# TensorE held to the program's order in layer 0, and sums of squares by head with the squares moving

## The chip, the cores and the metric

The kernel runs on one core of one Trainium2 chip. The metric is the device time of one execution in microseconds (us), the median of three runs. The trace is one profiled execution. Engines are named as in the profile: PE is TensorE's matmuls and PEld its weight loads, DVE is VectorE, ACT ScalarE, POOL GpSimd, SP SyncE; a q behind a name (ACTq, SPq) is the engine's queue, which issues DMAs. L12 is line 12 of the kernel before.

## The reference, cut to what matters

A first block of two layers works on x (256 tokens, width 1024): windowed attention (even layer), then latent attention with rotary keys (odd layer), a final RMS norm. A second block of two layers then works on x and on a context ctx of 256 tokens. In each of its layers:

- an RMS norm over the width and a modulation computed from c;
- q, k and v; **q and k are normalised per head half** (64 channels), the attention's output per head (128 channels), so sums of squares by head are needed;
- differential attention, x over x and ctx; a pooling and a convolution branch; gates; an output projection;
- an expert layer (`peer_ffn`): 8 heads each choose 16 of 16384 experts by two top-16 lists over 128 keys; `gelu(x . u_e)` times the gate weighs the row `v_e`.

```python
def rms_norm(x, g):
    xf = x.astype(jnp.float32)
    y = xf * lax.rsqrt(jnp.mean(xf * xf, axis=-1, keepdims=True) + EPS)
    return (y * g.astype(jnp.float32)).astype(x.dtype)

def qk_heads(p, g):
    b, l = p.shape[:2]
    return rms_norm(p.reshape(b, l, N_HEADS, 2, HEAD_DIM), g)

def attn_out_norm(o, g, lam_init):
    b, l = o.shape[:2]
    return (rms_norm(o, g) * (1.0 - lam_init)).reshape(b, l, ATTN_W)
```

## The kernel before, in words

**Layout.** Activations lie transposed: channels on the 128 partitions, 256 tokens along the free axis, eight chunks for 1024 channels. Most matrices come in chunks of 128x1024 (512 KB). `WS` (L253) loads each by DMA (L268), splits it into a high part (`wa`, ACT, L281) and a low part (`wb`, DVE, L282), up to LEAD chunks ahead, and `mm3` (L405) multiplies with three passes (high x high, high x low, low x high): 24 matmuls a chunk at L409 to L411. Chunks named in `whole` are not split and take 8 matmuls in full precision (`mm1`, L413, L416).

**Order of the work.** The program is a set of Python generators. Each yields a number of units, roughly its share of time, and combinators interleave them: `lead` (L1654) runs side generators by a rate against the main one, `par` (L1623) shares by weights, `along` (L1679) steps a side once per unit over a rate, `until` (L1671) runs a generator up to a `yield None`. What they settle is the order of writing. The framework then **schedules**: for each engine, DMA queues included, it plays the program on a model of the chip and picks the next instruction among those that are ready by that model, earlier-written ones first. It also assigns the buffers (42 of 4 KB under the tag `pg`) in that order. The order on an engine is fixed before the run; on the chip each engine works through its own.

**Stages.** `program` (L1699) starts with x's first norm (in `b1`, L693), ctx's norm and the first modulation matmuls (`mods`, L537, L574). Then two streams run side by side under `lead`, ctx at twice x's units (RATE[0]): x goes through the first block (`b1`), then layer 0's mixer; ctx goes through its mixer (`mixer`, L1160: `qkv`, `attn2`, branches, output), its choice of experts (`topk`, L1223), layer 1's modulation, and from about 860 us on through `rows` (L1351): each chosen expert's row is gathered by an indirect DMA (L1381), multiplied and added on DVE (L1392, L1401); 512 such rows, paced by units. At 1290 us x's mixer ends and `ffn_start` (L1690) begins: 24 steps (SOLO) of the choice alone, then under `par` the rest of the choice, the **G tables** (`gbuild`, L1470: one-hot products per token, L1487 and L1489 on DVE, L1495 on PE, written to DRAM at L1504 from ACT's queue) and the first 20 chunks of expert matrix u (`peer`, L1507, up to its `yield None`; 16 in full precision, four split: NPRE). A full-precision chunk counts 256/75 = 3.41 units, a split one 256/100 = 2.56. From 1560 to 2300 us `peer`'s main loop takes 128 chunks of u (the first ones done) and v. Layer 1 follows in the same pattern without ctx's mixer.

**Norms.** `rms_bcast` (L464) squares on ACT (L472), sums over channels with PE: ones as 32-column weights, squares moving, chunk k of four into the 32 output partitions of column group k (L474). A copy (L476), two matmuls by token (L479), the reciprocal root on DVE (`rsqrt`, 13 small operations, L396 to L403), a diagonal tile (L498) and a product with ones (L501) spread it over the partitions. The sums **by head** go another way: in `qkv` (L946) and `attn2` (L1046) each 128x128 block of squares is the stationary operand, and two columns (`sel2`) or one (`ones`) move. `rows_hl` (L895) then transposes the reciprocal roots (L905 in qkv, L903 in attn2), and L966 and L1056 spread them.

**Attention** runs in units: `first` (scores, softmax), `second` (transposes of p, L656 and L1015), `third` (product with v), written as first(i), second(i-1), third(i-2) (`attn_causal` L623, `attn2` L984).

Instructions at one line can show as two in the trace: a full-precision matmul counts twice.

Of the kernel before, what the change touches and what calls it, by code (L numbers as in the profile page):

```python
# [18 lines left out]
T = 256  # L19
# [15 lines left out]
NPRE = (16, 20), (20, 28)  # L35
# [16 lines left out]
for _name, _w in (("ident", 128), ("iota", 128), ("perm", 128), ("sel2", 2),  # L52
                  ("ropeC", 256), ("ropeS", 256), ("edge", 64), ("causal", 256),
                  ("iota16", 16), ("starts", 16), ("fold", 32), ("misc", 8)):
    _C[_name] = (_n, _n + _w)
    _n += _w
# [10 lines left out]
def const_tables():  # L67
# [11 lines left out]
    perm = np.zeros((128, 128), np.float32)  # L79
    perm[p ^ 32, p] = 1.0  # L80
    put("perm", perm)
    put("fold", np.concatenate([np.eye(32, dtype=np.float32)] * 4, 0))
    put("sel2", np.stack([p < 64, p >= 64], 1).astype(np.float32))
# [209 lines left out]
class Ker:  # L293
# [169 lines left out]

    def rms_bcast(s, hch, n):  # L464

        nc = s.nc
        st = s.ps("m")
        if n == 8:

            for g in range(0, n, 4):  # L470
                sq = s.pg([128, 4, T], F32, "sq")
                nc.scalar.activation(sq, hch(g, 4), AF.Square)  # L472
                for k in range(4):
                    nc.tensor.matmul(st[32 * k:32 * k + 32, :T], s.ones[:, 0:32], sq[:, k], start=g == 0, stop=g == 4)  # L474
            gs = s.s1([128, T], "gs")
            nc.scalar.copy(gs, st[:, :T])  # L476
            ss = s.ps("m")
# [26 lines left out]
    def rms(s, h, n=8):  # L504
        rbs = s.s1([128, T], "rbs")
        s.nc.vector.tensor_copy(rbs, s.rms_bcast(lambda g, m: h.t[g // 4][:, :], n))
        return rbs

    def norm_hl(s, h, a, b, name, n=8, rbs=None):

        nc = s.nc
        rbs = rbs if rbs is not None else s.rms(h, n)
        o = HL(s, name, n)
        for k in range(n):
# [6 lines left out]
            else:  # L521
                nc.scalar.activation(oh, y, AF.Identity, bias=b(k))
                nc.vector.scalar_tensor_tensor(ol, y, b(k), oh, op0=OP.add, op1=OP.subtract)
        return o

    def norm_f(s, h, a, b, o):

        nc = s.nc
        rbs = s.rms(h)
        for k in range(8):  # L530
            y = s.s1([128, T], "ny")
            nc.vector.scalar_tensor_tensor(y, h.ch(k), a(k), rbs, op0=OP.mult, op1=OP.mult)
            nc.scalar.activation(o.ch(k), y, AF.Identity, bias=b(k))  # L533
        return o
# [88 lines left out]
    def attn_causal(s, scores, bias, init, scale, val, emit):  # L623
# [69 lines left out]
    def b1(s, x, eng, out):  # L693
# [8 lines left out]
        hn = s.norm_hl(x, lambda k: s.V("norm_w", k), None, "hn")  # L702
        del x
        ws.load(W1)
        yield 1.0
# [81 lines left out]
        hn = s.norm_hl(x, lambda k: s.V("norm_w", 8 + k), None, "hn")  # L787
# [48 lines left out]
        cqn = s.norm_hl(cq, lambda k: s.V("cqn", k), None, "cqn", 2)  # L836
        ckn = s.norm_hl(ckv, lambda k: s.V("ckvn", k), None, "ckn", 1)
# [49 lines left out]
        rb = s.rms_bcast(lambda g, m: x.t[g // 4][:, :], 8)  # L887
# [7 lines left out]
    def rows_hl(s, rr, lo, n):  # L895
# [12 lines left out]
        nc.vector.tensor_tensor(rl[z], tb[z, :T], rh[z], op=OP.subtract)  # L908
        return rh[z], rl[z]


    def qkv(s, l, hn, ws, rope, want_q, r):
# [36 lines left out]
        s.rsqrt(rr, bank[:, :2 * nc_].rearrange("p (a b) -> p a b", a=2), 1.0 / 64, hv, t)  # L949
# [3 lines left out]
        rh, rl = s.rows_hl(rr, 0, 16)  # L953
        yield 8.0
# [29 lines left out]
    def attn2(s, l, q, kv, sr, o):  # L984
# [45 lines left out]
        for i in range(18):  # L1030
            if i < 16:
                first(i)
            if 1 <= i < 17:
                second(i - 1)
            if i >= 2:
                third(i - 2)
            yield 3.0

        bank = s.ps("m")
        for hf in range(2):  # L1040
            sq = s.pg([128, 4, T], F32, "sq")
            nc.scalar.activation(sq, o.t[hf], AF.Square)
            for k in range(4):
                for tt in range(2):
                    f = tt * 8 + hf * 4 + k
                    mm(bank[:, f:f + 1], sq[:, k, tt * 128:(tt + 1) * 128], s.ones[:, 0:1], start=True, stop=True)  # L1046
        rr, hv, t = (s.rq([128, 2, 8], nm) for nm in ("rr", "rhv", "rt2"))
        s.rsqrt(rr, bank[:, :16].rearrange("p (a b) -> p a b", a=2), 1.0 / 128, hv, t)
        z = slice(64, 72)
        rh, rl = s.rows_hl(rr, 64, 8)  # L1050
        yield 4.0
# [108 lines left out]
    def mixer(s, l, st, src, ws, eng, res, kvx, late=None, before=None, seq=False, h=None, rbs=None, side=None):  # L1160
# [7 lines left out]
        hn = s.norm_hl(h, lambda k: s.a1[l][:, k, st:st + 1], m0, "hn", rbs=rbs)  # L1168
# [50 lines left out]
        res["xn"] = s.norm_f(h, lambda k: s.a2[l][:, k, st:st + 1], s.mod(l, st, 3), Act(s, F32, "xn"))  # L1219
# [3 lines left out]
    def topk(s, l, xn, ws, eng, res, rows=False):  # L1223
# [8 lines left out]
        for h, sb in s.lin(ws, xn, 16):  # L1232
            if sb is None:
                yield 2.6
                continue
            qf = s.s2([128, 512], "qf")
            nc.scalar.copy(qf, sb)
# [17 lines left out]
            if h % 4 < 3:  # L1255
                continue
# [38 lines left out]
            for j in range(2):  # L1295
                for hf in range(2):
# [13 lines left out]
                    yield TY  # L1310
        ts = tp[:, 2].rearrange("p h t k -> p (h t) k")
# [158 lines left out]
    def gbuild(s, res, G, eng, ntc=8):  # L1470
# [7 lines left out]
        iob = io[:, None, :, :].to_broadcast(sh)  # L1478
        for tc in range(ntc):
            gt = [s.pg([128, 32, 32], F32, "gt") for _ in range(4)]  # L1480
            for q in range(4):
# [8 lines left out]
                for u in range(2):  # L1490
                    bank = s.ps("m")
                    for i in range(4):
                        t = u * 4 + i
                        for j in range(2):
                            mm(bank[:, i * 128:(i + 1) * 128], hot[:, 0, t // 2, :, t % 2], gat[:, j, t // 2, :, t % 2],  # L1495
                               start=j == 0, stop=j == 1)
                    for jq in range(4):
                        o = q * 8 + u * 4
                        nc.scalar.activation(gt[jq][:, :, o:o + 4],  # L1499
                                             bank.rearrange("p (t j) -> p j t", t=4)[:, jq * 32:(jq + 1) * 32, :],  # L1500
                                             AF.Copy, scale=1.0 / GS)
                    yield 1.0
            for jq in range(4):
                eng.dma_start(G[jq * 8:(jq + 1) * 8, :, tc].rearrange("g p j t -> p g (j t)"),  # L1504
                              gt[jq].rearrange("p (g j) t -> p g (j t)", g=8))
# [184 lines left out]
def ffn_start(k, l, rx, ws, G, pe, tot, *more, ntc=8):  # L1690

    eng = k.nc.gpsimd
    tk = k.topk(l, rx["xn"], ws, eng, rx)
    for i in range(SOLO):
        yield next(tk, None)
    yield from par(k, (chain(tk, lambda: k.gbuild(rx, G, k.nc.scalar, ntc)), TG), (until(pe), tot), *more)


def program(k, upto):  # L1699
    nc, ai, ao = k.nc, k.ai, k.ao  # L1700
    sy, gp = nc.sync, nc.gpsimd
    x = [k.h_load(ai["xT"].rearrange("a p k t -> a p (k t)"), sy, "x")]
    k.setup()
    ctx0 = ai["ctxT"].rearrange("a p k t -> a p (k t)")
# [63 lines left out]
```

## Time and profile before

| | |
|---|---|
| Median of three runs | 3698.21 us (3693.96 to 3700.71) |
| The profiled execution's own time | 3691.09 us |
| Its span, first to last instruction | 3689.3 us |
| Mean granted TensorE clock | 0.932 of 2.4 GHz |
| PE, PEld, DVE, ACT, POOL busy | 88%, 80%, 76%, 40%, 25% |
| Moved by DMA | 941.10 MB, 255 GB/s in the mean |

The profile's page gives totals; its windows give, for a stretch of the span, each engine's busy time, the granted clock (1.00 is 2.4 GHz, 0.50 is 1.2 GHz) and the DMA engines' busy share. A wait row names the waiting engine, line and tile, and what released it. In a timeline row the first number is the start, the second the length, and brackets hold the idle time before it with its releaser. The end of a matmul is modelled, so a busy PE is not PE at its peak.

### The profile page before, as it was taken

Reading aid. Unit: us, or ns where it says so; the run is one execution under the profiler, and the core shown is the slowest. Engines: PE = TensorE matmul, PEld = TensorE weight load, DVE = VectorE, ACT = ScalarE, POOL = GpSimd, SP = SyncE. Lnnn points to the kernel's source line nnn. Section 1 sums busy time; section 2 is a strip of 40 time slices with the busy share of each in tenths; the row PEclk is TensorE's granted clock in tenths of the full one; section 3 lists DMA queues with packets and bytes.
Section 4 is the critical chain, followed back from the end, with each engine's and each line's share of the span. In section 5 each row is a group of like instructions: output and inputs, shape, how many; then the busy total and the mean of one; then the engine's idle time right before and its main releaser. Section 6 shows DMA issues by size and latency. Waiting matters only on the chain. (4 is left out here: it accounts for less than half of the span.)

```text
span 3689.3 us, 61049 instructions
## 1 busy us (share of the span) xinstructions
PE 3258.1 (88%) x23324; PEld 2966.9 (80%) x23324; DVE 2790.7 (76%) x5722; ACT 1485.0 (40%) x2785; POOL 935.6 (25%) x831
## 2 busy tenths in 40 slices
PE   6989989996799885679999999778998689999999
PEld 5976889766689774668888888767988589999999
DVE  4356585578899889799989999788465978777655
ACT  3444345323355313333443444333353154444443
POOL 2002101212343512365555555232000003111000
PEclk9989999998899897889999999888999899999999
DMA  8536446756688845999999999776525089888764
GB/s 298 160 126 215 146 138 189 274 183 225 238 299 280 321 161 181 344 408 386 384 379 386 379 387 381 248 280 231 158 88 192 12 262 354 307 285 286 263 217 153
DMA packets 315430, 941.10 MB, mean 255 GB/s; under 512 B 29616, under 2 KB 93136, under 8 KB 315136
## 3 DMA queue, kind: packets, MB, share of 16 engines
q1 hardware_dynamic: 130848, 468.77, 35.7%
q0 software_dynamic: 118816, 432.76, 32.3%
q10 hardware_dynamic: 65472, 35.66, 3.2%
q8 instruction: 183, 3.00, 0.3%
q14 instruction: 111, 0.91, 0.1%
HBM read 893.01 MB, written 43.02 MB: 254 GB/s over the span
## 5 line engine op out<-in xcount | busy, mean ns | idle before, releaser
L282 DVE TENSOR_TENSOR wb<-wr,wa 128x1024 fp32r<-128x1024 f32 x846 | 1015.4, 1222 | 321.5 <-ACT wa L281 304.9
L281 ACT CAST wa<-wr 128x1024 fp32r<-128x1024 f32 x846 | 856.3, 1046 | 108.3 <-DMA wr<-in_w 39.0
L409 PE MATMUL pu<-hnh,wa 128*128 128x256 f32 x2000 | 586.0, 293 | 47.9 <-ACT wa L281 45.9
L411 PE MATMUL pu<-hnh,wb 128*128 128x256 f32 x2000 | 583.4, 293 | 17.1 <-DVE wb L282 17.0
L410 PE MATMUL pu<-hnl,wa 128*128 128x256 f32 x2000 | 578.5, 290 | 0.0
L409 PE MATMUL pu<-xh,wa 128*128 128x256 f32 (+1 forms) x1760 | 492.1, 280 | 10.1 <-ACT wa L281 9.6
L1381 POOL DMA_INDIRECT row<-in_pu,ridx x256 | 365.1, 1426 | 520.7 <-DVE wb L282 124.5
L410 PE MATMUL pu<-xl,wa 128*128 128x256 f32 (+1 forms) x1760 | 491.2, 279 | 0.9 <-DVE xl L1538 0.9
L411 PE MATMUL pu<-xh,wb 128*128 128x256 f32 (+1 forms) x1760 | 491.4, 279 | 0.0
L1381 POOL DMA_INDIRECT row<-in_pv,ridx x256 | 354.4, 1384 | 473.5 <-DVE wb L282 133.0
L409 PEld LDWEIGHTS pu<-hnh,wa 128*128 128x128 f32 x2000 | 397.7, 199 | 65.0 <-ACT wa L281 52.0
L411 PEld LDWEIGHTS pu<-hnh,wb 128*128 128x128 f32 x2000 | 395.8, 198 | 32.5 <-DVE wb L282 21.9
L410 PEld LDWEIGHTS pu<-hnl,wa 128*128 128x128 f32 x2000 | 397.4, 199 | 3.9 <-issue 3.5
L409 PEld LDWEIGHTS pu<-xh,wa 128*128 128x128 f32 x1760 | 338.5, 192 | 20.1 <-ACT wa L281 14.5
L410 PEld LDWEIGHTS pu<-xl,wa 128*128 128x128 f32 x1760 | 338.5, 192 | 4.6 <-DVE xl L1538 1.1
L411 PEld LDWEIGHTS pu<-xh,wb 128*128 128x128 f32 x1760 | 338.5, 192 | 1.8 <-issue 0.4
L1401 DVE SCALAR_TENSOR_TENSOR racc<-row,rwg,racc 128x1024 f32<-128x1024 f32 x254 | 325.5, 1282 | 0.4
L416 PE MATMUL pu<-xn,wr 128*128 128x256 f32 (+1 forms) x1344 | 311.9, 389 | 4.7 <-ACT xn L533 4.7
L1392 DVE CUSTOM_DVE_ANT_0 row<-row,xr 128x1024 f32<-128x1024 f32 x256 | 311.2, 1221 | 0.0
L1528 ACT ACTIVATE gel<-pu 128x256 f32<-128x256 f32 (+1 forms) x208 | 77.2, 371 | 577.8 <-PE pu L411 553.0
L416 PEld LDWEIGHTS pu<-xn,wr 128*128 128x128 f32 x1344 | 261.6, 199 | 41.7 <-issue 6.2
L1570 PE MATMUL pm<-W,wa 128*128 128x224 f32 x1024 | 276.1, 275 | 1.6 <-ACT wa L281 1.6
(427 smaller groups left out, 6487.7 us busy)
## 6 DMA issues: line engine op xcount, KB each, us to landing
wr<-in_w SPq DMA_DIRECT2D x288, 512.0 KB
wr<-in_pu SPq DMA_DIRECT2D x256, 512.0 KB
wr<-in_pv SPq DMA_DIRECT2D x256, 512.0 KB
wr<-in_w POOLq DMA_DIRECT2D x130, 512.0 KB
wm<-in_wmod POOLq DMA_DIRECT2D x96, 512.0 KB
G<-gt ACTq DMA_DIRECT2D x60, 512.0 KB
gp<-G SPq DMA_DIRECT2D x32, 512.0 KB
gp<-G SPq DMA_DIRECT2D x32, 448.0 KB
```

The costliest lines, as they stand in the source:

```text
L281: nc.scalar.copy(a, r)
L282: nc.vector.tensor_tensor(b, r, a, op=OP.subtract)
L409: mm(out, ah, bh, start=i == 0, stop=False)
L410: mm(out, ah, bl, start=False, stop=False)
L411: mm(out, al, bh, start=False, stop=i == n - 1)
L416: s.nc.tensor.matmul(out, w[:, k * 128:(k + 1) * 128], x(k), start=k == 0, stop=k == 7)
L1381: nc.gpsimd.indirect_dma_start(out=t, out_offset=None, in_=tab[w], in_offset=bass.IndirectOffsetOnAxis(ap=s.ridx[:, tt, i:i + 1], axis=0))
L1392: v.tensor_tensor_reduce(t, t, xr[tt], 1.0, 0.0, OP.mult, OP.add, hid[:, i:i + 1])
L1401: v.scalar_tensor_tensor(out[tt], t, wg[:, i:i + 1], out[tt], op0=OP.mult, op1=OP.add)
L1528: nc.scalar.activation(g, bank[:, :NT], AF.Gelu_apprx_tanh)
L1570: mm(o, vh[:, c], W[:, 0], start=j == 0 and d % 2 == 0, stop=False, skip_group_check=True)
```

## The change

Six edits belong together.

1. TensorE keeps the order of writing (`manual_schedule` with PE alone) from the start to the end of layer 0's `ffn_start`; the other engines' orders stay the scheduler's, and so does everything behind.
2. The generators get more and finer steps: the norms yield between their parts (and so are written among the other stream's steps), ctx's first norm is written beside x's, and attention is written first(i), second(i-2), third behind it, with nearly the same total of units.
3. The sums of squares by head use `rms_bcast`'s way: selector columns (`hs`, `ho`, 32 wide) are stationary, the squares move with 256 columns, four column groups. A copy (`grouped`) and two matmuls by token (`by_token`, selectors `hp`, `hq`) bring them to the old layout. This holds in both layers.
4. `topk` and `gbuild` get a skewed form, used in layer 0: a head's selection is written behind the next head's projection, a group's table matmuls behind the next group's one-hot work.
5. `ffn_start` in layer 0 writes expert chunks at six units for each unit of the choice behind its first 24 steps (EARLY), then the tables and the remaining chunks with weights 64 and 50. The early chunks' units no longer count for the pace of the rows. Layer 1 keeps the old form.
6. NPRE of layer 0 goes from (16, 20) to (20, 24).

```diff
-NPRE = (16, 20), (20, 28)
+NPRE = (20, 24), (20, 28)
+EARLY = 6.0, 50.0
...
+    hs, hp = np.zeros((128, 62), np.float32), np.zeros((4, 32, 32), np.float32)
+    ho, hq = np.zeros((128, 33), np.float32), np.zeros((4, 32, 8), np.float32)
+    hs[:64, 30], hs[64:, 31], ho[:, 1] = 1.0, 1.0, 1.0
...
+    def grouped(s, st):
+        gs = s.s1([128, T], "gs")
+        s.nc.scalar.copy(gs, st[:, :T])
+        return gs
+
+    def by_token(s, gs, w):
+        n = w.shape[1]
+        o = s.ps("m")[:, :2 * n].rearrange("p (a b) -> p a b", a=2)
+        for tt in range(2):
+            s.nc.tensor.matmul(o[:, tt], gs[:, tt * 128:(tt + 1) * 128], w, start=True, stop=True)
+        return o
...
                 nc.scalar.activation(sq, hch(g, 4), AF.Square)
+                yield 1.5
...
             nc.scalar.copy(gs, st[:, :T])
+            yield 1.0
...
             nc.vector.tensor_scalar(dg[:, tt], s.C("ident"), r[:, tt:tt + 1], None, op0=OP.mult)
+        yield 4.0
...
-        for i in range(18):
+        for i in range(19):
             if i < 16:
                 first(i)
-            if 1 <= i < 17:
-                second(i - 1)
-            if i >= 2 and i % 2 == 1:
-                third((i - 3) // 2)
-            yield 1.7
+            if 2 <= i < 18:
+                second(i - 2)
+            if i >= 4 and i % 2 == 0:
+                third((i - 4) // 2)
+            yield 1.6
...
-        bank = s.ps("m")
-        nc_ = 16 * len(todo)
+        nc_, sqs = 16 * len(todo), []
         for a, off, _ in todo:
             for hf in range(2):
-                sq = s.pg([128, 4, T], F32, "sq")
-                nc.scalar.activation(sq, a.t[hf], AF.Square)
-                for k in range(4):
-                    f = (0 if off else 16) + 2 * (hf * 4 + k)
-                    for tt in range(2):
-                        mm(bank[:, tt * nc_ + f:tt * nc_ + f + 2], sq[:, k, tt * 128:(tt + 1) * 128], s.C("sel2"),
-                           start=True, stop=True)
+                sqs.append((s.pg([128, 4, T], F32, "sq"), 30 - (0 if off else 4) - 2 * hf))
+                nc.scalar.activation(sqs[-1][0], a.t[hf], AF.Square)
+            yield 1.0
+        bank = s.ps("m")
+        for n, (sq, f) in enumerate(sqs):
+            for k in range(4):
+                mm(bank[32 * k:32 * k + 32, :T], s.C("hs")[:, f:f + 32], sq[:, k],
+                   start=n == 0, stop=n == len(sqs) - 1)
+        del sqs, sq
+        gs = s.grouped(bank)
+        yield 1.0
+        bank = s.by_token(gs, s.C("hp")[:, :nc_])
...
+        prev = None
+        for h, sb in s.lin(ws, xn, 16):
+            if sb is None:
+                yield 2.6
+                continue
+            qf = s.s2([128, 512], "qf")
+            nc.scalar.copy(qf, sb)
+            if not skew:
+                yield from select(h, qf)
+                continue
+            if prev is not None:
+                yield from select(*prev)
+            prev = h, qf
...
-def ffn_start(k, l, rx, ws, G, pe, tot, *more, ntc=8):
+def ffn_start(k, l, rx, ws, G, pe, early, tot, ntc=8):
     eng = k.nc.gpsimd
-    tk = k.topk(l, rx["xn"], ws, eng, rx)
+    tk = k.topk(l, rx["xn"], ws, eng, rx, skew=bool(early))
     for i in range(SOLO):
         yield next(tk, None)
-    yield from par(k, (chain(tk, lambda: k.gbuild(rx, G, k.nc.scalar, ntc)), TG), (until(pe), tot), *more)
+    pre = until(pe)
+    if not early:
+        gb = lambda: k.gbuild(rx, G, k.nc.scalar, ntc, skew=False)
+        yield from par(k, (chain(tk, gb), TG), (pre, tot))
+        return
+    yield from lead(tk, (pre, early))
+    yield from par(k, (k.gbuild(rx, G, k.nc.scalar, ntc), 64.0), (pre, tot))
...
+    with k.tc.manual_schedule(engines={mybir.EngineType.PE}):
...
+        def norm_ctx():
+            rbc.append((yield from k.rms(hc[0])))
+        drain(par(k, (until(b1), 1.0), (norm_ctx(), 1.0)))
...
+        drain(along(ffn_start(k, 0, rx, ws, k.G[0], pe, *EARLY), rows, RATE[2]))
     rx.clear()
     drain(along(pe, rows, RATE[3]))
```

## Rows read from the trace of the kernel before

**Rows 1.** Page: busy time, share of the span and instructions by engine

```profile
PE 3258.1 (88%) x23324; PEld 2966.9 (80%) x23324; DVE 2790.7 (76%) x5722; ACT 1485.0 (40%) x2785; POOL 935.6 (25%) x831
```

**Rows 2.** Windows: length, PE, PEld, DVE, ACT, POOL busy, clock, DMA share, GB/s

```profile
100.00:860.00 760.00, 695.59 (x4782) 592.96 (x4781) 470.39 (x1458) 300.13 (x578) 103.42 (x193) 0.92 0.52 176
860.00:1290.00 430.00, 376.46 (x2757) 352.35 (x2755) 372.48 (x632) 187.11 (x288) 171.11 (x125) 0.92 0.81 284
...
1340.00:1415.00 75.00, 29.70 (x156) 25.70 (x155) 72.62 (x336) 7.80 (x21) 4.34 (x3) 0.70 0.14 43
1415.00:1532.00 117.00, 90.80 (x711) 77.05 (x708) 107.61 (x165) 52.20 (x268) 35.91 (x27) 0.87 0.90 297
...
1560.00:2300.00 740.00, 673.72 (x4007) 595.57 (x4008) 685.38 (x911) 299.68 (x466) 411.52 (x284) 0.97 0.99 386
```

**Rows 3.** TensorE's waits, 100 to 860 us: total, times, longest

```profile
PE pm L501 <- DVE dg L498: 22.9, 5, 10.1
PE pm L656 <- DVE p L649: 10.4, 4, 3.9
...
PE pm L474 <- ACT sq L472: 6.6, 3, 4.6
...
PE pm L1015 <- DVE nb L1002: 2.5, 1, 2.5
```

**Rows 4.** TensorE's waits, 860 to 1290 us

```profile
PE pm L905 <- DVE rr L403: 12.4, 1, 12.4
...
PE pm L501 <- DVE dg L498: 3.0, 1, 3.0
```

**Rows 5.** Groups by line, the squares by head: count, busy us, mean ns, idle before

```profile
L946 PE MATMUL pm<-ct,sq 128*128 128x2 f32 x224 | 31.4, 277 | 0.0
...
L1046 PE MATMUL pm<-ones,sq 128*128 128x1 f32 x96 | 14.5, 284 | 0.0
```

**Rows 6.** One short window behind the first squares by head

```profile
170.00:175.00 5.00, 5.00 (x24) 5.00 (x25) 2.12 (x6) 0.91 (x1) 0.00 (x0) 0.50 0.34 105
```

**Rows 7.** Timeline of TensorE, layer 1's x stage

```profile
2423.26 9.00 PE L946 MATMUL pm<-ct,sq 128*128 128x2 f32 x64
...
2458.48 0.63 PE L905 MATMUL pm<-ct,rr 128*16 128x128 f32 x2
```

**Rows 8.** Line L474: shortest, median, longest ns

```profile
L474 PE MATMUL pm<-sq,ones x160: 379/403/636, 5.5 to 2828.8; 128*32 128x256 f32 x160
```

**Rows 9.** Timeline, two norms over the model dimension: start, us, idle before in brackets

```profile
850.94 1.08 PE L474 MATMUL pm<-sq,ones 128*32 128x256 f32 x8 [4.58 <-ACT sq L472]
...
859.29 0.77 PE L501 MATMUL pm<-dg,ones 128*128 128x128 f32 x2 [4.20 <-DVE dg L498]
...
1283.52 0.64 PE L474 MATMUL pm<-sq,ones 128*32 128x256 f32 x8 [1.54 <-issue]
1284.22 0.37 ACT L476 COPY gs<-pm 128x256 f32<-128x256 f32 x1 [0.76 <-PE pm L474]
...
1284.65 0.81 PE L479 MATMUL pm<-ct,gs 128*128 128x1 f32 x4 [0.49 <-ACT gs L476]
```

**Rows 10.** Timeline, ends of the choice and of the G tables

```profile
1402.29 0.47 PE L1344 MATMUL pm<-ct,tt 128*128 128x128 f32 x1 [32.03 <-ACT tt L1343]
...
1533.00 10.08 ACTq L1504 DMA_DIRECT2D G<-gt  x3
...
1544.30 0.58 PE L409 MATMUL pu<-xh,wa 128*128 128x256 f32 x1 [9.63 <-ACT wa L281]
...
1560.91 1.71 PE L1578 MATMUL pm<-wa,W 128*128 128x512 f32 x4 [2.01 <-ACT wa L281]
```

**Rows 11.** Waits of the SP queue, 1340 to 1560 us

```profile
SPq L268 <- DVE top L1309: 43.8, 1, 43.8
```

**Rows 12.** Window of the start: the same columns as rows 2

```profile
24.50:33.00 8.50, 8.50 (x58) 8.40 (x54) 5.95 (x22) 2.47 (x5) 1.96 (x4) 1.00 1.03 418
```

**Rows 13.** Timeline of TensorE at the start

```profile
52.27 0.58 PE L409 MATMUL pu<-hnh,wa 128*128 128x256 f32 x1 [6.08 <-ACT wa L281]
```

More of the change, by code (lines that the diff above doesn't have):

```diff
@@ L511, in norm_hl @@
         nc = s.nc
-        rbs = rbs if rbs is not None else s.rms(h, n)
+        if rbs is None:
+            rbs = yield from s.rms(h, n)
         o = HL(s, name, n)
@@ L528, in norm_f @@
         nc = s.nc
-        rbs = s.rms(h)
+        rbs = yield from s.rms(h)
         for k in range(8):
@@ L886, in b1 @@
         s.dump("x2", x)
[L887 removed]
+        rb = yield from s.rms_bcast(lambda g, m: x.t[g // 4][:, :], 8)
         for k in range(8):
@@ L1231, in topk, with select @@
         IX = s.sml([128, 8, 4, 16], "topi", H16, bufs=1)
[L1232 to L1237, printed above, removed]
+        def select(h, qf):
             sb = s.ps("m")
@@ L1478, in gbuild, with tables @@
         iob = io[:, None, :, :].to_broadcast(sh)
+        def tables(hot, gat, gt, tc, q):
+            for u in range(2):
+                bank = s.ps("m")
+                for i in range(4):
+                    t = u * 4 + i
+                    for j in range(2):
+                        mm(bank[:, i * 128:(i + 1) * 128], hot[:, 0, t // 2, :, t % 2], gat[:, j, t // 2, :, t % 2],
+                           start=j == 0, stop=j == 1)
+                for jq in range(4):
+                    o = q * 8 + u * 4
+                    nc.scalar.activation(gt[jq][:, :, o:o + 4],
+                                         bank.rearrange("p (t j) -> p j t", t=4)[:, jq * 32:(jq + 1) * 32, :],
+                                         AF.Copy, scale=1.0 / GS)
+                yield 1.0
+            if q < 3:
+                return
+            for jq in range(4):
+                eng.dma_start(G[jq * 8:(jq + 1) * 8, :, tc].rearrange("g p j t -> p g (j t)"),
+                              gt[jq].rearrange("p (g j) t -> p g (j t)", g=8))
+        prev = None
         for tc in range(ntc):
@@ L1489, in gbuild @@
                     v.tensor_tensor(gat[:, j], hot[:, 1], w[2 + j], op=OP.mult)
[L1490 to L1505, printed above, removed]
+                if not skew:
+                    yield from tables(hot, gat, gt, tc, q)
+                    continue
+                if prev is not None:
+                    yield from tables(*prev)
+                prev = hot, gat, gt, tc, q
+        if skew:
+            yield from tables(*prev)
     def peer(s, l, xn, G, eng, eng2, nnat, npre, out, keep=None, NT=T, rows=None):
@@ L1701, in program @@
     sy, gp = nc.sync, nc.gpsimd
-    x = [k.h_load(ai["xT"].rearrange("a p k t -> a p (k t)"), sy, "x")]
-    k.setup()
-    ctx0 = ai["ctxT"].rearrange("a p k t -> a p (k t)")
-    hc = [k.h_load(ctx0, sy, "hc")]
-    rc, rx = {}, {}
-    x3, cn, acc = [], [], []
-    b1 = k.b1(x.pop(), sy, x3)
-    next(b1)
-    rbc = [k.rms(hc[0])]
-    md = k.mods(0, gp)
-    drain(until(md))
-    wc = WS(k, ai["w2"][0], gp, whole=WHOLE)
-    def choose():
-        yield from k.topk(0, rc["xn"], wc, gp, rc, rows=True)
-        cn.append(rc.pop("xn"))
@@ L1718, in program @@
-    rows = k.rows(cn, acc)
-    ws = WS(k, ai["w2"][0], sy, whole=WHOLE)
-    ctx = chain(k.mixer(0, 1, ctx0, wc, gp, rc, lambda: [], md, seq=True, h=hc.pop(), rbs=rbc.pop()),
-                lambda: par(k, (choose(), 69.0), (k.mods(1, gp), 26.0)))
-    xs = chain(b1, lambda: k.mixer(0, 0, k.hd["x"], ws, sy, rx, lambda: [k.kv_load(sy)], seq=SEQ, h=x3.pop()))
-    drain(lead(xs, (chain(ctx, lambda: scaled(rows, RATE[0] / RATE[1])), RATE[0]), (k.setup2(), 0.5)))
-    kp = {}
-    pe = k.peer(0, rx["xn"], k.G[0], sy, sy, *NPRE[0], k.hd["x"], kp)
```

116 lines of the change are left out of this document (79 added, 37 removed).

## The prediction

> **What bounds the kernel now.** I read the page first: TensorE is busy 88% of the span, VectorE 76% [rows 1]. An average over such different stages decides nothing, so next comes the table by stage [rows 2]. The reader should see four kinds of stage. From 100 to 860 us two streams of work, x and ctx, share TensorE: busy 695.59 of 760 us, no other engine near its limit, so 64.4 us idle, at a mean granted clock of 0.92. From 860 to 1290 x is alone with the gathered rows: TensorE idles 53.5 of 430 us, but VectorE is busy 372.48. In the choice (1340 to 1415) VectorE is busy 72.62 of 75 us and TensorE 29.70; in the G tables (1415 to 1532) VectorE 107.61 of 117. From 1560 to 2300 the DMA share is 0.99. What TensorE's order can buy is therefore mainly in the first two stages; in the choice and the tables it can only move work out of what follows.
>
> Next come TensorE's waits in those two stages [rows 3, 4]. The largest are ends of norm chains: the product with the diagonal tile at L501 waits 22.9 us for VectorE and the squares at L474 wait 6.6; the softmax transposes at L656 wait 10.4 and at L1015 2.5. In the x-alone stage one wait of 12.4 us (L905, transposes of the reciprocal roots) is the largest. Last come the squares' totals and single instructions, and those at the ends of the choice and the tables [rows 5 to 13].
>
> **The change, part by part.** The sum is made against the profiled execution, 3691.09 us with a span of 3689.3; the median shown is 3698.21, 7.1 more, added at the end.
>
> *Squares by head.* Before, each 128x128 block of squares is loaded as weights and two or one columns move: 224 and 96 instructions (two per matmul), together 31.4 + 14.5 = 45.9 us of TensorE [rows 5]. They sit in seven places: four in qkv and three in attn2. After, the squares move, 256 columns, over four column groups, as L474 does already: a set of four matmuls (8 instructions) takes 0.64 us at full clock and 1.08 at half [rows 9]. The new code has 4 + 4 + 2 + 4 sets in qkv and 3 x 2 in attn2, 20 in all: 20 x 0.64 = 12.8 us. Each place gains a copy (L476's 0.37 us on ScalarE) and two matmuls by token (L479's 0.81): 7 x 1.18 = 8.3. So 45.9 - 21.1 = 24.8 us less, whether TensorE is the bound or stands at the end of the chain, since both squares and hop lie in the chain to the reciprocal root. **Taken: -25.** One end: if VectorE's queue sets the chain anyway, nothing is gained and the hop costs +8; layer 1's x stage looks so, its transposes start 26 us after the squares end [rows 7]. The other end is -35: during the narrow squares, which run from 164 to 174 us, the granted clock falls to 0.50, the lower of the two levels, 1.2 GHz [rows 6]; with 256 columns moving it may stay up, and some 10 us at the lower level behind each of two such places would be worth about 5 us each. I take neither end, being nearest to the rows that only add durations.
>
> The Trainium skill ("TensorE: Matmul & The Clock Gate", Part 3: Packing small matmuls) puts a pack of column tiles at the duration of one matmul plus some 4 ns for each further tile. With the shortest single L474 instruction, 0.379 us [rows 8], that estimate is 20 x 0.39 = 7.8 us in place of 12.8, and the gain 5 us larger; the row of a whole set, 0.64 us, contradicts it as long as a set stands by itself, and the row is what I use.
>
> *TensorE in program order, 100 to 860.* The scheduler's order waits where its model took a chain for finished. Program order puts the other stream's pieces there by the written steps: new steps inside the norms, transposes two units behind the scores instead of one. The waits these steps address are at L501, L474, L656 and L1015: 22.9 + 6.6 + 10.4 + 2.5 = 42.4 us [rows 3]. **Taken: half, -21.** All of it would be -42, and the clock could add to it (0.92 over 760 us is 61 us of full clock not granted [rows 2]; a quarter back, -15); the other end is a loss, priced in the second rival.
>
> *x alone, 860 to 1290.* Here no second stream fills a chain; branches and attention still alternate. Program order can no longer put a later chunk ahead of a waiting chain. **Taken: +5**, with -10 (the 12.4 us wait at L905 goes) and +30 (three chains of 10 us without cover) as ends.
>
> *Choice and G tables.* The choice's last transposes come after a TensorE idle time of 32.03 us, while VectorE works [rows 10]. After, ten or so of now 24 expert chunks are written before these transposes (6 units for each of the choice's last six; the 24 cost 20 x 3.41 + 4 x 2.56 = 78.5 units, 36 go early). This cannot shorten the choice or the tables, which VectorE sets. It can shorten 1532 to 1560, where the four split chunks run behind the tables with a wait of 9.63 us for their cast. Against that, ScalarE's queue issues G writes for 10.08 us and loads of the expert weights stand behind G's read, so the first product at 1560.91 has a chain of its own [rows 10]. A load of weights waited 43.8 us for VectorE in this stage [rows 11]; if that remains, the early chunks hold up the transposes. **Taken: -12**, ends 0 and -28. Of the gathered rows, the units of this stage fall from 57.8 of the choice + 64 of the tables + 64.9 of the chunks to 60.4 + 64 + 42.5, as early chunks no longer count; at 0.25 rows a unit that is 47 before and 42 after. The five come later at the same price: nothing. The skewed tables keep two more tiles per group: nothing, while tiles are free.
>
> *Peer phase.* Four more chunks done ahead: 4 x 0.524 MB less at 386 GB/s [rows 2] in the stage that DMA sets. **Taken: -5**, ends 0 and -6. Their shorter TensorE work (full-precision chunks instead of split) is hidden by the DMA.
>
> *Start.* The first chunk of q ran ahead of the modulation matmuls and filled 24.5 to 33 us; its place is now behind them, 8 us. But then the wait of 6.08 us for the next cast goes [rows 12, 13]. **Taken: +2**, ends -3 and +8. *Layer 1* keeps the scheduler's order; its skewed attention: nothing, ends -3 and +5.
>
> Sum: -25 - 21 + 5 - 12 - 5 + 2 = -56, so 3691 - 56 = 3635, and with 7 for the median **3642 us**.
>
> **Rivals.** *Order worth nothing (0.18).* The scheduler's order was as good: the 64 us stay, and G's writes set the table stage. Left are the squares, the peer phase and the losses of the x-alone stage and the start: 3691 - 25 - 5 + 5 + 2 + 7 = 3675. For it: from 100 to 860 us TensorE is busy 92% of the time as it is [rows 2]. Against: the waits of rows 3 are at known chain ends.
>
> *Program order pays every chain (0.17), the slower side.* One waiting matmul stops all behind it on TensorE. Behind 100 us the region has 11 norm chains (seven of rms, two of qkv, two of attn2); today TensorE waits in them 22.9 + 6.6 us up to 860 and 12.4 + 3.0 after [rows 3, 4], some 4 us each, because other matmuls run meanwhile. One bare chain is 8.4 us from squares to diagonal product (850.94 to 859.29) [rows 9], and with rows on VectorE 12.4 us of wait alone. If each costs 10 us, that is 110 instead of 45, +65; with -25 - 12 - 5 + 2 left: 3691 - 40 + 65 + 7 = 3723. It decides from about 85 us of waits in these chains, where the gains are used up. The Trainium skill (same page and part) states that matmuls start and end strictly in order, only weight loads being pulled ahead; the trace agrees, with nothing of TensorE's running during the 12.4 us [rows 4]. The mechanism and its price stand without that sentence.
>
> *Squares worth nothing as well (0.10).* VectorE's queue sets the chains, the hops add 8, order gains only in the choice: 3691 + 8 - 12 - 5 + 2 + 7 = 3691, within the bound of the median shown.
>
> **How the numbers follow.** The forecast has 0.55, its own range 3600 to 3675. About 0.2% (7 us) is what a measurement tells from no change. Faster: the forecast and the first rival, 0.73. Same: 0.10. Slower: 0.17. The range goes from 3580 (3642 with the further 10 of the squares, 21 of the order, 16 of the choice and 15 of the clock; 0.08 left below) to 3723, the middle of the slower case (0.09 above).
>
> **What would show it.** Right: squares on TensorE in the seven places at 13 us or less in sum; TensorE's waits for the diagonal tile between 100 and 860 at half of 22.9; expert chunks ahead of the choice's transposes; the peer phase's first product less than 25 us behind the last G matmul. Wrong: waits of 10 us or more in several norm chains, a longer stretch from 100 to 860, the clock there under 0.92, or the transposes waiting for a pu load.

## The result, and the profile after

The changed kernel takes **3640.35 us**, the median of four runs (3632.09 to 3646.42), beside 3697.47 for the kernel before: a ratio of **0.9844**, 95% interval 0.9823 to 0.9866. Its profiled execution took 3640.57 us, with a span of 3638.8. The time is the forecast's; the terms of the sum behind it are not, as the runs below show.

The table by stage comes first, with the same columns as in [rows 2], and the stages cut anew, so that each ends at the same event in every kernel: x's first product of layer-0 attention; the first of the choice's transposes; the peer phase's first product; its last one; the first transposes of layer 1's choice; the end. I call them A to F; A's end is set to within 1.5 us. The kernel before:

```profile
0.00:981.00 981.00, 861.92 (x5900) 738.58 (x5901) 607.63 (x1706) 378.58 (x686) 167.93 (x270) 0.91 0.58 202
981.00:1402.00 421.00, 353.84 (x2488) 328.31 (x2484) 374.24 (x991) 154.23 (x253) 139.40 (x101) 0.91 0.69 243
1402.00:1561.00 159.00, 110.54 (x847) 95.52 (x847) 134.11 (x212) 64.37 (x298) 47.57 (x36) 0.83 0.86 289
1561.00:2319.00 758.00, 690.91 (x4104) 610.43 (x4105) 702.70 (x934) 306.62 (x479) 419.66 (x291) 0.97 0.99 386
2319.00:2939.00 620.00, 518.83 (x3538) 478.76 (x3536) 443.56 (x1141) 221.71 (x343) 78.48 (x70) 0.89 0.50 172
2939.00:3689.00 750.00, 722.01 (x6454) 715.29 (x6453) 528.50 (x742) 359.51 (x729) 82.53 (x64) 0.98 0.78 261
```

The changed kernel, cut at the same events:

```profile
0.00:943.00 943.00, 818.75 (x5782) 693.70 (x5784) 614.56 (x1722) 380.90 (x689) 183.66 (x281) 0.92 0.62 216
943.00:1384.00 441.00, 377.65 (x2623) 349.34 (x2619) 385.31 (x1011) 159.15 (x261) 132.38 (x102) 0.92 0.68 244
1384.00:1528.00 144.00, 98.91 (x815) 87.36 (x813) 124.91 (x195) 62.68 (x294) 41.47 (x34) 0.82 0.86 279
1528.00:2292.00 764.00, 690.15 (x4007) 607.08 (x4008) 696.23 (x927) 302.50 (x471) 413.49 (x290) 0.95 0.98 383
2292.00:2885.00 593.00, 495.79 (x3488) 456.17 (x3486) 429.52 (x1124) 221.79 (x346) 74.24 (x60) 0.91 0.51 171
2885.00:3639.00 754.00, 723.69 (x6454) 716.56 (x6454) 528.90 (x743) 360.07 (x729) 82.56 (x64) 0.98 0.77 260
```

Stage by stage: -38, +20, -15, +6, **-27**, +4, together -50. The prediction had for E only layer 1's share of the squares, by its own prices some 10 of the 25 us, and it had a smaller loss in B.

Next the groups by line: the squares by head and their new hop.

```profile
L982 PE MATMUL pm<-sq,ct 128*32 128x256 f32 x112 | 9.8, 448 | 3.1 <-ACT sq L977 3.0
...
L488 PE MATMUL pm<-ct,gs 128*128 128x32 f32 (+2 forms) x28 | 4.6, 279 | 2.1 <-ACT gs L480 1.6 <-issue 0.5
L1088 PE MATMUL pm<-sq,ct 128*32 128x256 f32 x48 | 4.5, 472 | 1.8 <-issue 0.9 <-ACT sq L1083 0.9
```

That is 9.8 + 4.5 + 4.6 = 18.9 us for 45.9 in [rows 5]: TensorE is relieved of 27.0 us, as the prediction worked it out (45.9 - 12.8 - 7 x 0.81 = 27.4).

TensorE's waits answer to [rows 3, 4]. First 100 to 780 us, where ctx now ends, then 780 to 943, then 943 to 1257:

```profile
PE pm L703 <- ACT pT L693: 7.3, 2, 6.7
PE pm L940 <- DVE rr L417: 7.3, 1, 7.3
PE pm L1056 <- DVE nb L1043: 5.9, 4, 3.3
PE pm L691 <- DVE p L684: 5.3, 3, 1.9
...
PE pm L940 <- DVE rr L417: 22.0, 1, 22.0
PE pm L503 <- ACT sq L500: 10.9, 2, 8.0
PE pm L533 <- DVE dg L529: 10.4, 2, 6.5
...
PE pm L938 <- DVE rr L417: 14.0, 1, 14.0
```

While both streams run, no wait for the diagonal tile (L533 now) is left among the larger ones; it was 22.9 us. But the stretch that both streams share ends at 780 and not at 860, and behind it x stands alone in three norm chains: one by head costs a single wait of 22.0, and two over the model dimension cost 10.9 at their squares and 10.4 at their diagonal tiles, in two waits each.

Last the timeline of TensorE at the ends of the choice and the tables:

```profile
1371.81 12.25 PE L430 MATMUL pu<-xn,wr 128*128 128x256 f32 x56
...
1385.59 1.39 PE L1404 MATMUL pm<-ct,tt 128*128 128x128 f32 x5 [1.42 <-ACT tt L1403]
...
1508.16 2.72 PE L1545 MATMUL pm<-gat,hot 128*128 128x128 f16 x24 [1.38 <-ACT gt L1549]
1528.17 2.08 PE L1651 MATMUL pm<-wa,W 128*128 128x512 f32 x4 [17.30 <-ACT wa L295]
```

Expert chunks now fill what was 32.03 us of idle time before the transposes [rows 10], and the first product comes 17.3 us behind the last G matmul. Of the signs that the prediction named as right, these two are there and so is the shorter wait for the diagonal tile; the squares, 9.8 + 4.5 = 14.3 us, missed their 13 by a little. Of the signs named as wrong one is there too, single waits above 10 us, though only where x stands alone. What each is worth, the signs don't say.

### The profile page after: what moved, and what is told of

The parts are those of the page before. It is cut to its first block, busy times and chain, and to the rows that moved or that the text cites. A ratio compares the mean times of both kernels' runs of the same rounds, so it can differ in the third digit from the quotient of the medians.

```text
span 3638.8 us, 60652 instructions
## 1 busy us (share of the span) xinstructions
PE 3204.9 (88%) x23160; PEld 2910.2 (80%) x23160; DVE 2779.4 (76%) x5718; ACT 1487.1 (41%) x2788; POOL 927.8 (25%) x831
## 5 line engine op out<-in xcount | busy, mean ns | idle before, releaser
L425 PE MATMUL pu<-hnh,wb 128*128 128x256 f32 x2000 | 579.7, 290 | 23.0 <-DVE wb L296 22.9
L1441 POOL DMA_INDIRECT row<-in_pu,ridx x256 | 352.8, 1378 | 541.3 <-DVE wb L296 118.4
L424 PE MATMUL pu<-xl,wa 128*128 128x256 f32 (+1 forms) x1728 | 483.8, 280 | 2.3 <-DVE xl L1611 2.3
L425 PE MATMUL pu<-xh,wb 128*128 128x256 f32 (+1 forms) x1728 | 483.7, 280 | 0.0
L430 PE MATMUL pu<-xn,wr 128*128 128x256 f32 (+1 forms) x1408 | 324.2, 388 | 3.4 <-ACT xn L567 3.4
L430 PEld LDWEIGHTS pu<-xn,wr 128*128 128x128 f32 x1408 | 274.1, 199 | 43.8 <-issue 7.5
```

The costliest lines, as they stand in the source:

```text
L424: mm(out, ah, bl, start=False, stop=False)
L425: mm(out, al, bh, start=False, stop=i == n - 1)
L430: s.nc.tensor.matmul(out, w[:, k * 128:(k + 1) * 128], x(k), start=k == 0, stop=k == 7)
L1441: nc.gpsimd.indirect_dma_start(out=t, out_offset=None, in_=tab[w], in_offset=bass.IndirectOffsetOnAxis(ap=s.ridx[:, tt, i:i + 1], axis=0))
```

## The experiments

Twelve kernels, each timed in five rounds. The lengths of stages A to F are cut as above, in each kernel's own trace; "rows" counts the gathered rows whose hidden products are still to be done when the peer phase has ended.

| kernel | ratio to before [interval] | A | B | C | D | E | F | rows |
|---|---|---|---|---|---|---|---|---|
| before | 1 | 981 | 421 | 159 | 758 | 620 | 750 | 20 |
| e1 squares alone | 0.9986 [.9976, .9996] | 970 | 423 | 162 | 759 | 613 | 755 | 19 |
| e5 and norm steps | 0.9864 [.9846, .9881] | 956 | 422 | 159 | 752 | 589 | 754 | 11 |
| e9 the same, fewer rows | 0.9943 [.9926, .9961] | 958 | 414 | 162 | 759 | 629 | 755 | 18 |
| e6 e5 and attention skew | 0.9807 [.9792, .9822] | 940 | 421 | 158 | 759 | 587 | 754 | 11 |
| e11 e6, more rows | **0.9780** [.9767, .9793] | 950 | 429 | 162 | 752 | 565 | 751 | 4 |
| e12 e6, x's new choice | 0.9798 [.9785, .9811] | 939 | 423 | 158 | 750 | 588 | 751 | 14 |
| e4 changed, no order | 0.9844 [.9831, .9857] | 943 | 427 | 158 | 754 | 595 | 754 | 15 |
| changed | 0.9844 [.9823, .9866] | 943 | 441 | 144 | 764 | 593 | 754 | 15 |
| e10 changed, old choice | 0.9839 [.9826, .9852] | 943 | 437 | 156 | 752 | 591 | 750 | 12 |
| e2 changed, old squares | 0.9860 [.9844, .9877] | 945 | 442 | 146 | 759 | 600 | 753 | 15 |
| e7 changed, fewer rows | 0.9835 [.9823, .9848] | 940 | 438 | 150 | 742 | 606 | 753 | 21 |
| e8 before, more rows | 0.9973 [.9962, .9984] | 983 | 425 | 161 | 760 | 595 | 751 | 12 |
| e3 before, in order | 1.0096 [1.0075, 1.0116] | 998 | 435 | 163 | 753 | 616 | 749 | 20 |

0.001 is 3.7 us. With each hidden row that is left for E an output row is left too. D varies from 742 to 764 us for nearly the same work, so a single profile says little about 10 us; the ratios decide.

**First set: the squares and the order, each alone and each left out.**

e1, on the kernel before:

```diff
-  mm(bank[:, f..], sq[:, k, tt], s.C("sel2"))
+  mm(bank[32 * k:32 * k + 32, :T], s.C("hs")[:, f:f + 32], sq[:, k])
+  gs = s.grouped(bank); bank = s.by_token(gs, s.C("hp"))
```

> The kernel before, with the new squares by head in both layers and nothing else of the change: the scheduler's order and the old steps stay. The prediction's term (45.9 us of squares become 12.8 us and 8.3 us of hops) gives -25 us: 3672, ratio 0.993. If VectorE sets the chains in which the squares stand, the hops cost 8: 3705, ratio 1.002. If narrow squares also cost granted clock behind them, -35: 3662, ratio 0.9905, with a higher mean clock.

e2, on the changed kernel, all steps kept:

```diff
-  mm(bank[32 * k:32 * k + 32, :T], s.C("hs")[:, f:f + 32], sq[:, k])
+  mm(bank[:, f..], sq[:, k, tt], s.C("sel2"))
```

> The changed kernel with the old squares by head (squares as weights, two columns or one moving), all else of the change kept, the new steps and their units too. If the parts add up, it lies 25 us above the changed kernel: 3665, ratio to before 0.991. If the squares are worth nothing it equals the changed kernel: 3640, 0.9845. If the squares are nearly the whole gain it is 3690 or more, 0.998.

e3, on the kernel before:

```diff
+    with k.tc.manual_schedule(engines={mybir.EngineType.PE}):
         x = [k.h_load(...)]
...
         drain(along(ffn_start(...), rows, RATE[2]))
```

> The kernel before, with TensorE held to program order up to layer 0's choice and tables, and no new steps: no step inside the norms, transposes one unit behind the scores, old squares. A theory that the program order by itself is what gains gives -20 to -30: 3670 to 3678, ratio 0.993 to 0.995. The prediction's second rival (each chain paid in full where no other stream's piece is written into it) gives +30 to +65 here: 3728 to 3763, ratio 1.008 to 1.018. If order is worth nothing either way, 3697.

e4, on the changed kernel:

```diff
-    with k.tc.manual_schedule(engines={mybir.EngineType.PE}):
+    if True:
```

> The changed kernel without the program order for TensorE: the scheduler's own order, with the new steps, squares, skewed choice and tables and 20 early chunks. If the order is worth the prediction's 21 + 12 - 5 - 2 = 26 us, 3666, ratio to before 0.9915. If the new steps alone bring it (more rows of the gathered work inside layer 0), it equals the changed kernel, 3640, 0.9845. If the scheduler's order is better once the steps are there, below 3635.

The squares are worth 5 us alone (0.9986) and 6 in the changed kernel (0.9860 against 0.9844, within the intervals), not 25. The page of e1, beside [rows 1], shows what became of them:

```profile
PE 3234.2 (88%) x23192; PEld 2934.0 (80%) x23192; DVE 2790.4 (76%) x5722; ACT 1485.5 (40%) x2792; POOL 927.3 (25%) x831
```

TensorE works 3258.1 - 3234.2 = 23.9 us less, and the span is 7.4 shorter. The rest became idle time. Around the first place the windows show it; the kernel before, then e1, both up to 200 us:

```profile
164.00:175.00 11.00, 11.00 (x73) 11.00 (x73) 4.03 (x7) 6.91 (x9) 0.00 (x0) 0.72 0.28 94
175.00:186.00 11.00, 11.00 (x43) 8.79 (x42) 4.59 (x14) 1.89 (x3) 0.00 (x0) 0.82 0.17 48
186.00:200.00 14.00, 14.00 (x82) 11.54 (x81) 6.34 (x20) 3.58 (x10) 1.06 (x2) 0.88 0.31 114
```

```profile
171.00:176.00 5.00, 5.00 (x25) 4.20 (x24) 2.44 (x6) 2.79 (x3) 0.00 (x0) 1.00 0.14 29
176.00:186.00 10.00, 10.00 (x68) 9.18 (x67) 4.89 (x14) 1.54 (x3) 0.00 (x0) 1.00 0.28 91
186.00:200.00 14.00, 9.86 (x54) 6.81 (x52) 10.02 (x30) 5.61 (x17) 1.06 (x2) 0.76 0.30 114
```

Before, TensorE is busy throughout, at a granted clock of 0.72 to 0.88. With the squares moving the clock stays at 1.00 up to 186 us; then TensorE idles 4.1 of 14 us while VectorE is busier than it was, and the clock falls to 0.76. The work that was saved had been covering the norm's chain. Layer 1's x stage shows the same in e1's timeline of TensorE:

```profile
2418.87 0.64 PE L967 MATMUL pm<-sq,ct 128*32 128x256 f32 x8
...
2453.87 0.38 PE L927 MATMUL pm<-ct,rr 128*16 128x128 f32 x2
```

The peer phase ends at 2314.5 there and at 2319.2 before, so the squares start 104 us behind it in both kernels, and the transposes that need them [rows 7] come 139 us behind it in both: nothing of the time saved on the squares reaches them.

The program order alone is 35 us slower (e3). The first two windows of e3, A and B:

```profile
0.00:998.00 998.00, 851.72 (x5848) 737.32 (x5850) 610.19 (x1706) 381.10 (x686) 167.49 (x270) 0.91 0.57 198
998.00:1433.00 435.00, 356.77 (x2509) 330.78 (x2505) 378.88 (x995) 154.64 (x251) 124.08 (x101) 0.90 0.66 235
```

TensorE idles 224.5 us in them, and 186.2 in the kernel before: the loss is waiting. In the changed kernel the order is worth nothing (0.9844 with it, and without it in e4). So neither of the two things that name this change makes the gain.

**Second set: what in the steps gains.**

e5, on e1: the new steps in norms, qkv and attn2, and the program's start as changed; the attentions, `NPRE` and the choice stay as before.

```diff
   nc.scalar.activation(sq, hch(g, 4), AF.Square)
+  yield 1.5
...
   nc.scalar.copy(gs, st[:, :T])
+  yield 1.0
```

> The kernel before with the new squares and the new steps inside norms, qkv and attn2, and the changed order of the program's start; the scheduler's order, the old attention skew, the old choice, tables and 16 early chunks. It stands between the squares alone (0.9986) and the changed kernel without program order (0.9844). If the steps are what gains, by the pieces of the other stream and the gathered rows that they let in, it is at 0.990 or less. If the gain lies in the attention skew or in the choice, it stays at 0.997 to 0.999.

e6, on e5:

```diff
-        for i in range(18):
+        for i in range(19):
...
-            if 1 <= i < 17:
-                second(i - 1)
+            if 2 <= i < 18:
+                second(i - 2)
```

> As the run before it, and with the attention transposes two units behind the scores. What is then missing to the changed kernel without program order is the skewed choice and tables and the 20 early chunks alone. The prediction's terms for these, 12 and 5 us, give 0.9844 + 0.0046 = 0.989; if they are the larger part, 0.993 or more; if nothing, 0.9845. The attention skew itself, against the run before it: 0 by the prediction for layer 1, up to -0.003 if the waits for the softmax (10.4 us and 2.5 us) go.

e7 on the changed kernel, e8 on the kernel before:

```diff
-RATE = 2.0, 0.32, 0.25, 0.45, 0.3, 2.0
+RATE = 2.0, 0.285, 0.25, 0.45, 0.3, 2.0
```

That is e7; in e8 the number is 0.36.

> The changed kernel with the pace of the gathered rows in layer 0 at 0.285 for 0.32 rows, which should put back as many of them inside layer 0's mixer as the kernel before had (66 hidden rows for 73). If the changed kernel's shorter stage between the two peers' ends (192 us for 215) is those rows, the time goes up by some 20 us, ratio to before 0.990. If a row costs the same wherever it runs, as the prediction said, it stays at 0.9845.

> The kernel before with the pace of the gathered rows in layer 0 at 0.36 for 0.32, so about 74 hidden rows for 66 before the choice, nothing else. If the pace is a cause of its own, some -20 us, ratio 0.994 to 0.995. If the rows only move, 1.000. If they hold up x's own stage between 860 and 1290 us, where VectorE is busy 87%, up to 1.003.

The norm steps gain 45 us on top of the squares (0.9986 to 0.9864), and the attention skew another 21. The pace of the rows is a cause too: seven hidden rows more inside layer 0 gain the old kernel 10 us. In the changed kernel, taking them back loses nothing (0.9835); its E is 13 us longer, as that theory asks, but its D came out at 742 for 764.

**Third set: the pace within the steps, the choice, and the best version.**

e9 is e5 with the same line at 0.285, e11 is e6 with it at 0.36. e10, on the changed kernel:

```diff
-NPRE = (20, 24), (20, 28)
+NPRE = (16, 20), (20, 28)
...
-  k.topk(0, rc["xn"], wc, gp, rc, rows=True)
+  k.topk(0, rc["xn"], wc, gp, rc, rows=True, skew=False)
...
-  ffn_start(k, 0, rx, ws, k.G[0], pe, *EARLY)
+  ffn_start(k, 0, rx, ws, k.G[0], pe, None, NPRE[0][1] * 3.41)
```

e12, on e4:

```diff
-            yield from k.topk(0, rc["xn"], wc, gp, rc, rows=True)
+            yield from k.topk(0, rc["xn"], wc, gp, rc, rows=True, skew=False)
```

> The squares with the norm steps (0.9864) at a pace of 0.285 for 0.32, so that 66 hidden rows and not 73 run before the choice, as in the kernel before. It parts the steps' gain (0.9986 to 0.9864, 45 us) into the pace of the rows and the rest. If the pace is a part, as in the kernel before, where seven rows more gave 10 us (0.9973), it is at 0.989 to 0.992. If with the steps there the pace is worth nothing, as in the changed kernel (0.9835 with fewer rows, 0.9844 with more), it stays at 0.9864.

> The changed kernel, program order and all, with the old choice and tables: no skew in layer 0's choices and tables, 16 chunks and none early. Against the same without program order (0.9807): if the order is worth nothing, as between 0.9844 and 0.9844 with the new choice, it is at 0.981. If program order is what the early chunks were there for (the old choice leaves TensorE waiting in order behind VectorE), 0.985 or more. If the prediction's -12 and -5 us for choice and chunks hold in program order, 0.989.

> The best so far (squares, norm steps, attention skew; scheduler's order, old choice; 0.9807) with a pace of 0.36 for 0.32, so some 82 hidden rows for 73 before the choice. If a row is cheaper there than in the stage after the peer, as in the kernel before, 3 to 6 us per thousand less: 0.975 to 0.978. If the room beside layer 0's mixer is used up, 0.981 or more, with the stage from 940 to 1239 us longer by what the stage behind the peer is shorter.

> The changed kernel without program order (0.9844), with the skewed choice taken out for ctx, so that only x has the skewed choice and tables and the 20 early chunks. Against the same with the old choice for both (0.9807), it tells where the 14 us went that the new choice cost. If in the choice of ctx, which runs beside x's mixer (x's layer-0 norm came 10 us later), 0.981 to 0.982. If in x's choice, tables and chunks, 0.984 to 0.985.

e9 parts the steps' 45 us: 29 are the pace of the rows (0.9943 to 0.9864), 16 the rest. Each new step adds to x's units, and `lead` lets the gathered rows run at 0.32 of these; so seven more of them have their hidden product inside layer 0 (73 for 66), and fewer stand behind the peer phase. The same step of the pace is worth 10 us on the kernel before (e8), 10 on e6 (e11) and nothing in the changed kernel (e7), so the 29 hold for this pair only. Groups by line in that stage, the kernel before and e11:

```profile
L1392 DVE CUSTOM_DVE_ANT_0 row<-row,xr 128x1024 f32<-128x1024 f32 x20 | 24.3, 1217 | 0.0
```

```profile
L1452 DVE CUSTOM_DVE_ANT_0 row<-row,xr 128x1024 f32<-128x1024 f32 x4 | 4.9, 1216 | 0.0
```

The pairs that differ in the pace alone price a left-over hidden row, with its output row, in E: e5 to e9 40 us for seven, before to e8 25 for eight, e6 to e11 22 for seven, the changed kernel to e7 13 for six: 2 to 6 us each. The program and the timelines show why. In layer 1, ctx's norm, keys and values are written behind the last gathered row, and x's attention needs them:

```python
    def kv_ctx():
        yield from scaled(rows, RATE[5])
        k.rows_add(0, acc, kp)
...
        yield from k.qkv(1, hn, wc, False, False, rc)
```

The last row on VectorE and the first product of x's attention in layer 1, for the kernel before, the changed one and e11 (start, duration, line):

```profile
2538.30 1.27 DVE L1401 SCALAR_TENSOR_TENSOR racc<-row,rwg,racc 128x1024 f32<-128x1024 f32 x1
2680.96 1.14 PE L998 MATMUL pm<-k,q 64*128 64x256 f32 x8
...
2483.07 1.28 DVE L1461 SCALAR_TENSOR_TENSOR racc<-row,rwg,racc 128x1024 f32<-128x1024 f32 x1
2631.62 0.70 PE L1039 MATMUL pm<-k,q 64*128 64x256 f32 x2
...
2417.50 1.28 DVE L1461 SCALAR_TENSOR_TENSOR racc<-row,rwg,racc 128x1024 f32<-128x1024 f32 x1
2563.27 0.70 PE L1039 MATMUL pm<-k,q 64*128 64x256 f32 x2
```

The rows of both kinds that are left are 59, 50 and 29; counted from the peer phase's end (2319.2, 2292.5, 2293.1), the last of them ends after 220, 192 and 126 us, some 3 us a row, and the attention starts after 362, 339 and 270. In all 14 kernels it starts 139 to 152 us behind the last row. From the changed kernel to e11 the attention moves up by 69 us and E shrinks by only 28: behind the attention's start E takes 253 us in the one and 294 in the other, with TensorE busy for 218 and 265, so work that used to run before the attention then runs beside it.

The timeline of VectorE behind layer 1's squares in the changed kernel (start, duration, line) shows a second way in which rows get between:

```profile
2408.68 1.26 DVE L1461 SCALAR_TENSOR_TENSOR racc<-row,rwg,racc 128x1024 f32<-128x1024 f32 x1
...
2409.84 0.23 DVE L410 TENSOR_SCALAR rt<-pm 128x64 f32<-128x64 f32 x1
...
2415.45 1.29 DVE L1461 SCALAR_TENSOR_TENSOR racc<-row,rwg,racc 128x1024 f32<-128x1024 f32 x1
2416.65 0.20 DVE L411 TENSOR_SCALAR rr<-rt 128x64 int32<-128x64 int32 x1
...
2424.54 0.24 DVE L416 TENSOR_TENSOR rt<-rt,rhv 128x64 f32<-128x64 f32 x1
```

and TensorE's next step of that chain (start, duration, as above):

```profile
2439.91 0.38 PE L940 MATMUL pm<-ct,rr 128*16 128x128 f32 x2
```

Operations of 0.2 us, each the successor of the one before, stand in VectorE's queue between rows of 1.2 to 1.3 us and other work. The chain from the last squares (2402.9) to the transposes takes 37 us, with 26 before [rows 7]; of the 29 us by which these squares end earlier, 18.6 are left at the transposes. That VectorE's queue, and not TensorE, times these transposes is why the squares gain nothing at this place.

The new choice does two things. For x (skew, tables, 20 chunks) it gains 3 us without program order (0.9807 to 0.9798, within the intervals), and in program order the whole of it gains nothing (0.9839 to 0.9844). For ctx, whose choice takes the same code's default, it **loses 17** (0.9798 to 0.9844, e12 to e4). Program order costs 12 where the choice is the old one (e6 to e10), nearly all of it, by these two profiles, in B, 421 to 437. TensorE's waits in e10, 943 to 1380 us:

```profile
PE pm L1404 <- ACT tt L1403: 19.4, 1, 19.4
PE pm L1283 <- ACT qf L1360: 17.8, 8, 7.7
PE pm L938 <- DVE rr L417: 12.8, 1, 12.8
```

In e6, 940 to 1361 us:

```profile
PE pm L1283 <- ACT qf L1360: 7.5, 1, 7.5
...
PE pm L938 <- DVE rr L417: 0.6, 1, 0.6
```

The first two waits of e10 are in the choice and cost nothing there: from the product with the diagonal tile in the norm ahead of it (1264.7 in e10, 1247.0 in e6) to its transposes it takes 115 and 114 us. The loss lies ahead of that norm, where L938 stands. These transposes come 258 us behind A's end in both kernels, but e6 works on other matmuls in the 12.8 us that e10 waits, and e10 does that work later: from them to the norm it takes 64 us, and e6 49.

**A version that beats both**: e11, 3609.37 us, 0.9780 to the kernel before. It keeps the scheduler's order and the old choice, and takes from the change the squares, the norm steps and the attention skew, with a faster pace for the rows.

## Why the prediction was right, and which of its steps were not

The total was right by luck: errors of both signs met. By the runs, from the kernel before to the changed one without order and on to the changed one, each step a difference of two ratios: squares -5, norm steps -45, attention skew -21, x's choice -3, ctx's choice +17, program order 0: together -57. The sum had -56. The split depends on the order in which the parts are added: in program order the whole new choice costs 2 us (e10 to the changed kernel) and not 14, and the order costs 12 with the old choice and nothing with the new.

*Squares by head (-25, measured -5 to -6).* The count and the durations held: 18.9 us for the forecast's 20 sets and seven hops (18.5 on TensorE). The step that failed is "whether TensorE is the bound or stands at the end of the chain": the prediction took the value nearest to the rows of durations, while its own row of a chain that VectorE sets [rows 7] was the better guide. Its end of -35 by the clock fell as well: the dip left the squares and came back, 0.76, where TensorE then idled. On the packing rule of the Trainium skill ("TensorE: Matmul & The Clock Gate", Part 3: Packing small matmuls), the trace now has both cases: a set alone takes 0.64, two back to back 1.07, so the second adds 0.43 us, near the 0.39 that the prediction estimated by the rule.

```profile
2399.59 0.64 PE L982 MATMUL pm<-sq,ct 128*32 128x256 f32 x8
...
2401.82 1.07 PE L982 MATMUL pm<-sq,ct 128*32 128x256 f32 x16
```

*Program order, 100 to 860 (-21).* The size was about right for A, the cause wrong. The prediction took the order and the steps as one thing. A falls by 14 with the norm steps (e1 to e5) and by 16 with the attention skew (e5 to e6); the order itself adds 3 (e6 to e10), all in single profiles. The scheduler's order makes as good use of the steps. The order without the steps costs 35 us, within the +30 to +65 that the second rival's price gives for it, and TensorE idles 38 us more in A and B: that rival's mechanism is real. With the steps the loss falls to 12 us with the old choice (e6 to e10) and to nothing with the new one (e4 to the changed kernel). The first rival, order worth nothing, was right about the order, but it too put the steps' gain into the order, and so its 3675 is off.

*x alone (+5).* In program order it was paid at about half of the upper end, +30: B is 16 us longer in e10 than in e6, ahead of the choice's norm, and a chain by head waits 12.8 us without cover.

*Choice and tables (-12), peer phase (-5).* Every sign named for them came, and no time: in program order the pair is worth 0 (e10 against the changed kernel). Against e10, C is 12 us shorter, but B is 4 longer, D 12 and E 2, and single profiles can't part the spread of D from the chunks' doing. The five rows fewer of that stage didn't come as reckoned: by VectorE's trace 48 rows of both kinds run in it before and after. But "the same price: nothing" was wrong all the same: against e10, six rows of both kinds more are left for E (50 for 44), where a pair costs 2 to 6 us. The prediction also did not notice that ctx's choice is skewed by the same default.

*The pace of the rows (not in the sum).* The prediction counted units for the choice stage alone, and not those that the new steps add in layer 0. Between e9 and e5 it is 29 us, the largest single difference, though other pairs have 10, 10 and nothing. In the changed kernel's E it is five hidden and four output rows less (59 to 50): the attention that waits for the last row starts 22.7 us earlier behind the peer phase's end, of the 27 by which E is shorter.

*Left open.* Why fewer rows cost the changed kernel nothing (e7), where they cost 29 us with the steps alone: its D, 742 us at 394 GB/s, is the shortest of all, beside 764 at 383 in the changed kernel, and no run here tells whether that belongs to the pace. The -5 of the peer phase can't be told from that spread either. Nor is it settled how ctx's skewed choice loses 17 us: they are spread over A, B, D, E and F, 3 to 7 us each.

## What to carry to other kernels

Time saved on the engine that is busy 88% counts only where that engine, and not a chain through another engine's queue, sets the end: follow the result to its consumer before pricing it. When a change adds steps to a generator, look up every pace that counts those steps, since side work moves with them, and ask who waits for the last piece of that side work. And test an order written by hand against the scheduler's with the same steps: here the steps gained, and the order did not.

## What the runs showed of the hardware beyond that

The stage that moves the peer's weights ran at 383 to 394 GB/s and took 742 to 764 us in the five kernels that have 24 chunks done ahead, with 291 rows beside it in each: a spread of 3% between single executions. In one profile that hides any effect of 5 us, such as the prediction's term for the peer phase.
